# A planned order on one core: in the dilated attention, transposes of queries and keys are planned with a longer cost for the Newton steps ahead of them

## The chip, the cores and the metric

One Trainium2 chip, one of its cores. The metric is the device time of one execution of the whole program in microseconds (us). The profile records one execution; it calls the engines PE (TensorE; PEld is its weight load), DVE (VectorE), ACT (ScalarE), POOL (GpSimd) and SP (which issues the loads).

## The reference, cut to what matters

A two-layer decoder trunk on 256 tokens of width 1024, all in float32. Layer 0 is a half-step SwiGLU, then the dilated attention that this change is about, then another SwiGLU; layer 1 has the same shape with another attention. In the dilated attention three groups (dilations) each have queries, keys and values for 16 heads of 64, and queries and keys are normalized per head and rotated:

```python
def rms_norm(x, g):
    y = x * lax.rsqrt(jnp.mean(x * x, axis=-1, keepdims=True) + EPS)
    return y * g

qkv = (u @ w_qkv).reshape(b, s, N_DIL, 3, N_HEADS, HEAD_DIM)
for g in range(N_DIL):
    q = rope(rms_norm(qkv[:, :, g, 0], q_gain[g]))
    k = rope(rms_norm(qkv[:, :, g, 1], k_gain[g]))
    o, lse = dilated_attention(q, k, qkv[:, :, g, 2], DIL_WINDOWS[g], DIL_RATES[g])
# the three outputs are merged by softmax of their lse; then @ w_o
```

## The kernel before

Every float32 product is made as three products of split operands (high part of both, and the two mixed ones), so weights come in from HBM as tiles `st` of 1 MB, are rounded on ACT to `wh` (L387) and their remainder is made on DVE as `wl` (L413), six half tiles of each at a time. DVE also does the sums for the modulation (L393, one line of `w_ada` at a time) in between.

The dilated attention works on four heads at a time, so there are four rounds, called heads 0-3, 4-7, 8-11 and 12-15 below. In a round PE first projects queries and keys of group 0, then 1, then 2 (`project`: 48 matmuls of 512 columns, lines 849 to 851, into two PSUM tiles, one for each 128 tokens), then values of two groups (48 matmuls of 512 columns) and of the third (48 of 256 columns; the first round has these from earlier). After each projection of queries and keys `qk_task` runs: ACT squares the result (L860), DVE multiplies it by the rope tables (L890, L894), POOL adds the two halves (L895), DVE sums the squares by head (L864) and makes a first guess of the reciprocal root (L877, L879), POOL refines it in three Newton rounds of four small instructions each (L581, L584, L585, L586: 128x16 elements) and multiplies the rows by it (L938, one instruction for each 128 tokens), and then PE transposes the eight blocks (L906) and ACT copies them out of PSUM (L912, 128x2x128).

When all three groups of a round are transposed, its four units start (`dil_unit`: two pairs of heads by two halves of the queries). A unit makes scores on PE (L967, L969), adds mask and takes the maximum on DVE (L975, L980), exponentials on ACT (L983), the division on DVE (L989, L991), eight transposes on PE (L906 too), which ACT (L912, 128x512) and DVE (L914) copy out, and the product with values on PE (L1007). The units of one round stand between the projections of the next; those of the last round stand between its value projections and the first parts of the output projection (L466 to L468).

Every engine runs its instructions in the order in which they are written. That order is made while the program is built by a planner: `_Clock` holds a time `now` for PE and one for each of the others. A step of a task that is a generator says with `yield T` that its next step is due at T; `tick` moves `now` on by the cost of the matmuls just written and writes the steps that are due. `on(engine, ns, after)` adds a cost to an engine's time and gives back when it ends; `G(512)` adds 2.2 x 512 + 120 ns for POOL. Weights are split by the same planner (`fill`), when DVE and ACT are free by its times. For the transposes there are two PSUM tiles `tp`, for scores two (`sc`), for projections three (`mm`).

Of the kernel before, what the change touches and what calls it, by code (L numbers as in the profile page):

```python
# [223 lines left out]
class _Kernel:  # L224
# [194 lines left out]
    def fill(self):  # L419

        clk = self.clk
        while not self.hold:
            T = clk.now + self.slack
            if self.lows and self.lows[0][0][2] < clk.now + self.lag and clk.free["V"] < T:
                self.low()
# [6 lines left out]
            e = self.queue[self.qpos][0]  # L432
            if self.staged[self.qpos][1] > T:
                return
            if e[0] == "w":
                if len(self.halves) >= self.released + self.depth or clk.free["A"] > T:
                    return
            elif clk.free["V"] > T:
                return
# [159 lines left out]
    def modulated(self, gs, sh, timed=False):  # L599
# [22 lines left out]
        self.hold = False  # L622
        T = self.clk.on("V", 800 * KC, self.clk.now)
        self.clk.free["A"] = max(self.clk.free["A"], T)
# [294 lines left out]
    def qk_task(self, ps, q, k, g):  # L919

        nc = self.nc
        x = self.small(16, "qkx")
        R = []
        clk = self.clk
        sq = [self.head_squares(ps[tt], 8) for tt in range(TT)]
        for tt in range(TT):
            clk.A(512, clk.now)
            T = clk.G(512, clk.V(1280, clk.now))
            R.append(self.rope(ps[tt].rearrange("p (a r d) -> p a r d", r=4, d=HD),
                               self.dtab[g][:, 0, tt], self.dtab[g][:, 1, tt]).rearrange("p a r d -> p (a r) d"))  # L930
        for tt in range(TT):
            self.head_sums(x[:, tt * 8:(tt + 1) * 8], sq[tt])
            T = clk.V(512)
        rs = self.head_rstd(x, 16)
        T = clk.on("G", 1700, clk.on("V", 400, T))
        for tt in range(TT):
            T = clk.G(512)
            nc.gpsimd.tensor_tensor(out=R[tt], in0=R[tt],  # L938
                                    in1=rs[:, tt * 8:(tt + 1) * 8].unsqueeze(2).to_broadcast([P, 8, HD]),
                                    op=ALU.mult)  # L940
        yield T
        for tt in range(TT):
            c = slice(tt * P, (tt + 1) * P)
            self.transpose4((q[:, :, c], k[:, :, c]), R[tt].rearrange("p h d -> p (h d)"))
# [915 lines left out]
```

## Time and profile before

| | |
|---|---|
| runs of the kernel before | 1300.01, 1301.76 and 1302.33 us, median 1301.76 |
| the profiled execution's own time | 1301.44 us |
| its span, from the first to the last instruction | 1299.7 us |
| PE busy | 1219.7 us, 94% |
| DVE busy | 975.8 us, 75% |
| ACT busy | 646.0 us, 50% |
| POOL busy | 258.0 us, 20% |

The median is the middle of three runs without a profile; the rows further down are of one execution with the profile. Times in rows count from the start of its span, which is 1.7 us shorter than the execution's own time. A busy share is over the whole span, and an engine with a low share can still be the one that others wait for in one stage. The dilated attention stands in the rows from about 236 to 561 us.

### The profile page before, as it was taken

The page shows a single profiled execution, that of the slowest core. Times are in us where ns is not written, and L with a number is a line of the kernel's source. Part 1 is how long each engine was busy: PE and PEld are TensorE (multiplying, and loading weights), DVE is VectorE, ACT ScalarE, POOL GpSimd, SP SyncE. Part 2 cuts the span into 40 slices and gives each one's busy share as a digit, 9 for nine tenths or more (in the row PEclk, how much of TensorE's full clock was granted, in tenths as well). Part 3 has the DMA queues.
Part 4 walks back from the last instruction along what each step waited for, and adds up shares of the span by engine and source line. Part 5 has one row for each costly group of instructions (what it writes and reads, how often), then busy time and mean ns, then how long its engine had stood idle before and what let it go on. Part 6 is the DMA issues. An engine that isn't in the chain of part 4 may idle for free.

```text
span 1299.7 us, 23375 instructions
## 1 busy us (share of the span) xinstructions
PE 1219.7 (94%) x9373; PEld 1140.8 (88%) x9373; DVE 975.8 (75%) x1743; ACT 646.0 (50%) x1126; POOL 258.0 (20%) x356
## 2 busy tenths in 40 slices
PE   4799999789989898899999999999999889999998
PEld 3799999667777687799999999989998778999998
DVE  6799886866758677578888878878878997766652
ACT  4545454435445354456455446545435477654431
POOL 3480010462433525210000100030001353000000
PEclk9999999999899899899999999999999899999999
DMA  8889886543454534245988956776883003466650
GB/s 323 285 328 353 314 317 259 201 163 154 143 191 151 196 130 162 97 163 181 340 321 324 341 213 244 279 279 248 343 305 135 33 2 132 163 257 232 242 192 17
DMA packets 42733, 284.50 MB, mean 219 GB/s; under 512 B 5249, under 2 KB 6273, under 8 KB 9346
## 3 DMA queue, kind: packets, MB, share of 16 engines
q1 hardware_dynamic: 42626, 283.02, 58.9%
q8 instruction: 73, 1.20, 0.4%
q14 instruction: 34, 0.28, 0.1%
HBM read 281.96 MB, written 1.05 MB: 218 GB/s over the span
## 4 chain that ended last, share of the span: by engine, by line
PE 73%; DVE 12%; POOL 9%; ACT 3%; issue 2%; DMA 1%; SPq 0%; ACTq 0%; DVEq 0%; POOLq 0%
PE mm L466 18%; PE mm L467 18%; PE mm L468 18%; PE mm L849 3%; PE mm L850 3%; PE mm L851 3%; DVE wl L413 2%; POOL y L938 2%; PE tp L906 2%; POOL rs_t L584 2%; POOL rs_t L581 2%; POOL rs_y L586 2%; POOL rs_t L585 1%; DVE y L1455 1%; DVE st L393 1%
## 5 line engine op out<-in xcount | busy, mean ns | idle before, releaser
L413 DVE TENSOR_TENSOR wl<-st,wh 128x1024 fp32r<-128x1024 f32 x361 | 436.1, 1234 | 93.4 <-ACT wh L387 93.0
L387 ACT CAST wh<-st 128x1024 fp32r<-128x1024 f32 x361 | 369.0, 1049 | 133.8 <-PE mm L468 46.6
L466 PE MATMUL mm<-uh,wh 128*128 128x256 f32 x1304 | 364.6, 280 | 1.4 <-DVE y L738 1.4
L467 PE MATMUL mm<-uh,wl 128*128 128x256 f32 x1304 | 364.5, 280 | 0.0
L468 PE MATMUL mm<-ul,wh 128*128 128x256 f32 x1304 | 363.4, 279 | 0.0
L466 PEld LDWEIGHTS mm<-uh,wh 128*128 128x128 f32 x1304 | 245.0, 188 | 1.7 <-DVE y L738 1.6
L467 PEld LDWEIGHTS mm<-uh,wl 128*128 128x128 f32 x1304 | 245.1, 188 | 0.1
L468 PEld LDWEIGHTS mm<-ul,wh 128*128 128x128 f32 x1304 | 245.2, 188 | 0.0
L466 PE MATMUL mm<-y,wh 128*128 128x256 f32 x832 | 233.5, 281 | 0.1
L467 PE MATMUL mm<-y,wl 128*128 128x256 f32 x832 | 232.4, 279 | 0.0
L468 PE MATMUL mm<-y,wh 128*128 128x256 f32 x832 | 231.8, 279 | 0.0
L393 DVE CUSTOM_DVE_ANT_0 st<-st,cact 128x1024 f32<-128x1024 f32 x152 | 187.0, 1259 | 0.0
L466 PEld LDWEIGHTS mm<-y,wh 128*128 128x128 f32 x832 | 156.4, 188 | 1.1 <-issue 0.9
L467 PEld LDWEIGHTS mm<-y,wl 128*128 128x128 f32 x832 | 156.4, 188 | 0.0
L468 PEld LDWEIGHTS mm<-y,wh 128*128 128x128 f32 x832 | 156.4, 188 | 0.0
L849 PE MATMUL mm<-wh,uh 128*128 128x512 f32 (+1 forms) x336 | 137.1, 408 | 0.0
L850 PE MATMUL mm<-wl,uh 128*128 128x512 f32 (+1 forms) x336 | 132.4, 394 | 0.0
L851 PE MATMUL mm<-wh,ul 128*128 128x512 f32 (+1 forms) x336 | 131.7, 392 | 0.0
L524 POOL TENSOR_TENSOR y<-y 128x256 f32<-128x256 f32 x20 | 22.7, 1137 | 351.9 <-ACT y L505 351.9
L895 POOL TENSOR_TENSOR y<-y 128x512 f32<-128x512 f32 (+1 forms) x26 | 32.3, 1251 | 267.3 <-DVE y L894 157.2
L849 PEld LDWEIGHTS mm<-wh,uh 128*128 128x128 f32 x336 | 67.2, 200 | 14.2 <-issue 1.3
L851 PEld LDWEIGHTS mm<-wh,ul 128*128 128x128 f32 x336 | 66.9, 199 | 13.8
(254 smaller groups left out, 1622.0 us busy)
## 6 DMA issues: line engine op xcount, KB each, us to landing
st<-w_in SPq DMA_DIRECT2D x88, 1024.0 KB, 5.1
st<-w_ada SPq DMA_DIRECT2D x76, 1024.0 KB, 5.5
st<-w_out SPq DMA_DIRECT2D x44, 1024.0 KB, 6.4
st<-w_qk SPq DMA_DIRECT2D x24, 1024.0 KB, 4.9
st<-w_va SPq DMA_DIRECT2D x8, 1024.0 KB, 4.8
st<-w_o SPq DMA_DIRECT2D x8, 1024.0 KB, 4.9
st<-w_vb SPq DMA_DIRECT2D x4, 1024.0 KB, 5.5
st<-w_q SPq DMA_DIRECT2D x4, 1024.0 KB, 6.4
```

The costliest lines, as they stand in the source:

```text
L387: nc.scalar.copy(out=wh, in_=src)
L393: nc.vector.tensor_tensor_reduce(out=src, in0=src, in1=self.cact, scale=1.0, scalar=0.0, op0=ALU.mult, op1=ALU.add, accum_out=self.mod[:, ...
L413: (self.nc.gpsimd if eng == "G" else self.nc.vector).tensor_tensor(out=o, in0=src[:, c], in1=i.bitcast(F32), op=ALU.subtract)
L466: mm(out=out, lhsT=ah, rhs=bh, start=start, stop=False, **kw)
L467: mm(out=out, lhsT=al, rhs=bh, start=False, stop=False, **kw)
L468: mm(out=out, lhsT=ah, rhs=bl, start=False, stop=stop, **kw)
L581: eng.tensor_tensor(out=t, in0=y, in1=y, op=ALU.mult)
L584: eng.tensor_tensor(out=t, in0=t, in1=x, op=ALU.mult)
L849: mm(out=ps[tt], lhsT=uh[k][:, c], rhs=wh[:, o], start=k == 0, stop=False)
L850: mm(out=ps[tt], lhsT=uh[k][:, c], rhs=wl[:, o], start=False, stop=False)
L851: mm(out=ps[tt], lhsT=ul[k][:, c], rhs=wh[:, o], start=False, stop=k == KC - 1)
L895: (eng or nc.gpsimd).tensor_tensor(out=A, in0=A, in1=B, op=ALU.add)
```

## The change

One number in `qk_task` is changed. It is the planned cost in ns of the three Newton rounds on POOL, from which the planner works out when the transposes are due:

```diff
         rs = self.head_rstd(x, 16)
-        T = clk.on("G", 1700, clk.on("V", 400, T))
+        T = clk.on("G", 6100, clk.on("V", 400, T))
         for tt in range(TT):
             T = clk.G(512)
```

The planner's time for POOL is used for nothing else in this stage. With the later T the task's next step, eight transposes on PE and four copies on ACT, is written later, and what was written around it moves up. No instruction of PE is added or taken away. POOL's and SP's instructions keep their order.

The first place is ACT in the round of heads 0-3. Rows L860 are the squares of a projection, L387 splits of weights, L912 with 128x2x128 the copies behind the transposes of queries and keys, L1107 the copies of values. Before:

```order
L860 ACTIVATE y<-mm 128x512 x2
L387 CAST wh<-st 128x1024 x4
L912 COPY y<-tp 128x2x128 x4
L860 ACTIVATE y<-mm 128x512 x2
L387 CAST wh<-st 128x1024 x4
L912 COPY y<-tp 128x2x128 x4
```

And with the change:

```order
L860 ACTIVATE y<-mm 128x512 x2
L387 CAST wh<-st 128x1024 x4
L860 ACTIVATE y<-mm 128x512 x2
L387 CAST wh<-st 128x1024 x2
L912 COPY y<-tp 128x2x128 x4
L387 CAST wh<-st 128x1024 x2
L860 ACTIVATE y<-mm 128x512 x2
```

The squares of group 1 and one pair of splits stand ahead of the copies of group 0 now; on PE 18 matmuls of 512 columns moved ahead of the transposes of group 0, and 21 and 3 more stand ahead of those of groups 1 and 2.

The second place is PE where the units of heads 0-3 stand in the projections of heads 4-7, at the transposes of group 0 of heads 4-7. L849 to L851 are the projection, L967 and L969 the scores of a unit, L1007 its product with values. Before, where the first row L906 is of queries and keys and the second of a unit:

```order
L906 MATMUL tp<-ident,y 128x128 x8
L849 MATMUL mm<-wh,uh 128x512
L850 MATMUL mm<-wl,uh 128x512
L851 MATMUL mm<-wh,ul 128x512
L906 MATMUL tp<-ident,y 128x128 x8
L967 MATMUL sc<-y 128x256
L969 MATMUL sc<-y 128x128 x2
L967 MATMUL sc<-y 128x256
L969 MATMUL sc<-y 128x128 x2
L1007 MATMUL o<-y 64x128 x8
```

With the change, where the sixteen are the unit's eight and then those of queries and keys:

```order
L967 MATMUL sc<-y 128x256
L969 MATMUL sc<-y 128x128 x2
L967 MATMUL sc<-y 128x256
L969 MATMUL sc<-y 128x128 x2
L906 MATMUL tp<-ident,y 128x128 x16
L849 MATMUL mm<-wh,uh 128x512
L850 MATMUL mm<-wl,uh 128x512
L851 MATMUL mm<-wh,ul 128x512
L1007 MATMUL o<-y 64x128 x8
```

Both pairs of transposes stand together, behind the next unit's scores. ACT at the same place, before (L983 are the exponentials, L912 with 128x512 the copy of one half of a unit's transposes):

```order
L387 CAST wh<-st 128x1024 x2
L912 COPY y<-tp 128x2x128 x4
L912 COPY y<-tp 128x512
L983 ACTIVATE y,den<-y,nb 128x512 x2
L860 ACTIVATE y<-mm 128x512 x2
```

and with the change:

```order
L387 CAST wh<-st 128x1024 x2
L983 ACTIVATE y,den<-y,nb 128x512 x2
L912 COPY y<-tp 128x512
L912 COPY y<-tp 128x2x128 x4
L860 ACTIVATE y<-mm 128x512 x2
```

The next unit's exponentials stand ahead of both copies. The third place is PE at the transposes of group 2 of heads 4-7. Rows with 128x512 are the values of two groups, with 128x256 those of the third. Before:

```order
L850 MATMUL mm<-wl,uh 128x512
L851 MATMUL mm<-wh,ul 128x512
L906 MATMUL tp<-ident,y 128x128 x8
L849 MATMUL mm<-wh,uh 128x512
L850 MATMUL mm<-wl,uh 128x512
L851 MATMUL mm<-wh,ul 128x512
L849 MATMUL mm<-wh,uh 128x256
```

and with the change:

```order
L850 MATMUL mm<-wl,uh 128x256
L851 MATMUL mm<-wh,ul 128x256
L906 MATMUL tp<-ident,y 128x128 x8
L849 MATMUL mm<-wh,uh 128x256
L850 MATMUL mm<-wl,uh 128x256
```

The transposes stand behind the rest of the first value projection and behind 24 of the 48 matmuls of the second.

Counted in the same listing, this is PE's work between the end of the projection of a group and its transposes ("a" is a matmul of 512 columns, "b" one of 256, T eight transposes, S the scores and O the product of a unit):

| heads, group | before | with the change |
|---|---|---|
| 0-3, 0 | 36a | 54a |
| 0-3, 1 | 45a | 6a T 60a |
| 0-3, 2 | 45a | 18a T 30a |
| 4-7, 1 | 27a T 6a O | 3a T 21a O 33a |
| 4-7, 2 | 45a | 9a T 39a 24b |
| 8-11, 1 | 30a T 6a O | 30a T 9a O 18a |
| 8-11, 2 | 45a | 9a T 39a 33b |
| 12-15, 1 | 3a T 21a O 12a | 3a T 21a O 33a |
| 12-15, 2 | 42a | 9a T 39a 24b |

At the end of the stage the listing has 18 matmuls of the output projection between the last unit's transposes and its product before, and 3 with the change; behind that product the rest of the first three columns of the output projection follows in both.

## Rows read from the trace of the kernel before

**Rows 1.** The page's first part: busy time, share of the span and number of instructions by engine.
```profile
PE 1219.7 (94%) x9373; PEld 1140.8 (88%) x9373; DVE 975.8 (75%) x1743; ACT 646.0 (50%) x1126; POOL 258.0 (20%) x356
```

**Rows 2.** Who waited for whom, PE alone, in the stretch of the dilated attention: us in total, times, longest.
```profile
PE tp L906 <- POOL y L938: 34.3, 15, 7.6
```

**Rows 3.** Busy time by stretch (from:to, length, busy time and count of instructions by engine, granted clock of PE, share of the DMA engines, GB/s): the stage, and the 4 us behind its longest wait.
```profile
236.00:561.00 325.00, 288.64 (x1612) 233.81 (x1611) 221.79 (x402) 143.65 (x259) 135.08 (x192) 0.94 0.44 163
258.00:262.00 4.00, 3.43 (x12) 2.85 (x13) 0.10 (x1) 1.79 (x5) 1.52 (x2) 0.50 0.93 358
```

**Rows 4.** The timeline of PE at transposes of queries and keys: start, us, what, and in brackets the idle time before it and what ended it. Heads 0-3: the first three; 4-7: the next three; 8-11: two; 12-15: two.
```profile
258.57 2.11 PE L906 MATMUL tp<-ident,y 128*128 128x128 f32 x8 [7.60 <-POOL y L938]
...
278.14 0.66 PE L906 MATMUL tp<-ident,y 128*128 128x128 f32 x4 [3.24 <-POOL y L938]
...
295.35 0.66 PE L906 MATMUL tp<-ident,y 128*128 128x128 f32 x4 [2.81 <-POOL y L938]
...
348.56 2.12 PE L906 MATMUL tp<-ident,y 128*128 128x128 f32 x8 [3.03 <-POOL y L938]
...
369.80 0.66 PE L906 MATMUL tp<-ident,y 128*128 128x128 f32 x4 [3.23 <-POOL y L938]
370.80 0.65 PE L906 MATMUL tp<-ident,y 128*128 128x128 f32 x4 [0.34 <-POOL y L938]
...
428.20 0.66 PE L906 MATMUL tp<-ident,y 128*128 128x128 f32 x4 [1.56 <-POOL y L938]
...
448.77 0.66 PE L906 MATMUL tp<-ident,y 128*128 128x128 f32 x4 [3.24 <-POOL y L938]
...
508.63 2.12 PE L906 MATMUL tp<-ident,y 128*128 128x128 f32 x8 [3.44 <-POOL y L938]
...
527.01 0.66 PE L906 MATMUL tp<-ident,y 128*128 128x128 f32 x4 [3.16 <-POOL y L938]
```

**Rows 5.** The timeline of PE at full clock: the first and the last of 51 matmuls of 512 columns without a wait between them; the first and the last of 33 of 256 columns; and eight transposes, the first of six matmuls, the product of a unit, and the first of the next scores.
```profile
262.84 0.40 PE L849 MATMUL mm<-wh,uh 128*128 128x512 f32 x1
...
274.50 0.40 PE L851 MATMUL mm<-wh,ul 128*128 128x512 f32 x1
...
375.29 0.28 PE L849 MATMUL mm<-wh,uh 128*128 128x256 f32 x1
...
379.07 0.28 PE L851 MATMUL mm<-wh,ul 128*128 128x256 f32 x1
...
465.60 1.03 PE L906 MATMUL tp<-ident,y 128*128 128x128 f32 x8
466.39 0.48 PE L849 MATMUL mm<-wh,uh 128*128 128x512 f32 x1
...
467.95 1.09 PE L1007 MATMUL o<-y 128*64 128x128 f32 x16
468.98 0.70 PE L967 MATMUL sc<-y 64*128 64x256 f32 x2
```

**Rows 6.** The same behind two of the waits: the first and the last of 60 matmuls of 512 columns, and of 54.
```profile
350.32 0.78 PE L849 MATMUL mm<-wh,uh 128*128 128x512 f32 x1
...
366.17 0.40 PE L851 MATMUL mm<-wh,ul 128*128 128x512 f32 x1
...
510.40 0.78 PE L849 MATMUL mm<-wh,uh 128*128 128x512 f32 x1
...
523.46 0.39 PE L851 MATMUL mm<-wh,ul 128*128 128x512 f32 x1
```

**Rows 7.** The timeline of POOL: the first, the eighth and the ninth of the twelve Newton instructions for heads 0-3, group 0, and the product behind them; the first one and the product for heads 4-7, group 2.
```profile
247.04 1.12 POOL L581 TENSOR_TENSOR rs_t<-rs_y 128x16 f32<-128x16 f32 x1 [0.32 <-DVE rs_y L879]
...
255.14 1.07 POOL L586 TENSOR_TENSOR rs_y<-rs_t,rs_y 128x16 f32<-128x16 f32 x1
256.29 0.21 POOL L581 TENSOR_TENSOR rs_t<-rs_y 128x16 f32<-128x16 f32 x1
...
257.48 2.04 POOL L938 TENSOR_TENSOR y<-y,rs_y 128x512 f32<-128x512 f32 x2
...
359.92 1.15 POOL L581 TENSOR_TENSOR rs_t<-rs_y 128x16 f32<-128x16 f32 x1 [0.39 <-DVE rs_y L879]
...
368.70 2.04 POOL L938 TENSOR_TENSOR y<-y,rs_y 128x512 f32<-128x512 f32 x2
```

**Rows 8.** The timeline of DVE in the same stretches: the last splits of weights ahead of group 1 of heads 0-3, and the splits beside the Newton steps of heads 4-7, group 2, with the next one behind them.
```profile
253.77 2.36 DVE L413 TENSOR_TENSOR wl<-st,wh 128x1024 fp32r<-128x1024 f32 x2
...
359.77 2.38 DVE L413 TENSOR_TENSOR wl<-st,wh 128x1024 fp32r<-128x1024 f32 x2
...
364.38 2.38 DVE L413 TENSOR_TENSOR wl<-st,wh 128x1024 fp32r<-128x1024 f32 x2
...
374.21 2.36 DVE L413 TENSOR_TENSOR wl<-st,wh 128x1024 fp32r<-128x1024 f32 x2 [7.45 <-ACT wh L387]
```

**Rows 9.** The timeline of PE and ACT in heads 8-11, where a unit's transposes stand behind the next unit's scores, and ACT's copy behind that unit's exponentials.
```profile
400.88 0.70 PE L967 MATMUL sc<-y 64*128 64x256 f32 x2
...
402.49 1.09 PE L906 MATMUL tp<-ident,y 128*128 128x128 f32 x8
...
405.03 0.56 ACT L912 COPY y<-tp 128x512 f32<-128x512 f32 x1
...
405.64 1.09 PE L1007 MATMUL o<-y 128*64 128x128 f32 x16 [0.67 <-ACT y L912]
```

## The prediction

> **What bounds the kernel now.** The page first: PE is busy 94% of the span and no other engine over 75% [rows 1], so what can be won is PE's idle time and the time in which its clock is low. Next, who PE waits for, in the stage that the change touches. In the 325 us from 236 to 561, PE is busy 288.6 at a mean granted clock of 0.94 [rows 3], so 36.4 us are idle, and 34.3 of these are one wait, in 15 pieces: transposes of queries and keys wait for POOL's product L938 [rows 2]. Then the places. The timeline has nine of them: all three groups of heads 0-3, and groups 1 and 2 of the other rounds. The first costs 7.60 us, seven others about 3 us, one 1.56 with a second piece behind it [rows 4]. Behind each PE finds its clock lower: in the 4 us behind the longest wait the granted clock is 0.50, the 1.2 GHz level [rows 3]. Behind the dilated attention PE goes on with products that it is busy with nearly all the time, so a us won in the stage is a us of the kernel.
>
> What is late there is POOL. Twelve Newton instructions took 10.4 us for heads 0-3, group 0 (257.48 - 247.04) and 8.8 for heads 4-7, group 2 (368.70 - 359.92) [rows 7]; the planner had 1.7.
>
> **What the change does to the waits.** It removes no work. It puts more matmuls ahead of the transposes, so a wait shrinks by what moved ahead, as long as POOL is ready at the same time after its projection as before. Prices at full clock: a matmul of 512 columns (a) takes (274.50 - 262.84)/50 = 0.233 us, one of 256 (b) (379.07 - 375.29)/32 = 0.118, eight transposes (T) 466.39 - 465.60 = 0.79, a unit's product (O) 468.98 - 467.95 = 1.03 [rows 5]. Work before plus wait before is the time from the end of a projection until its product L938 is there; I call it the lag. Work between, by the table in the section on the change:
>
> - Heads 0-3, group 0: 36a (8.4) and 7.60. 18a more are 4.2, which leaves a wait of 3.4.
> - Group 1: 10.5 + 3.24 = 13.7. With the change 6a, that wait of 3.4, T and 60a stand between, over 19 us: no wait.
> - Group 2: 10.5 + 2.81, and about 1.0 that low clock cost within the 45a: 14.3. Now 18a T 30a = 12.0: a wait of 2.3. Nothing but these values can cover it, since the units need all three groups.
> - Heads 4-7, group 1: 9.5 + 3.03 = 12.5 against 15.1 now. Group 2: 10.5 + 3.23 = 13.7 against 14.8.
> - Heads 8-11: 10.2 + 1.56 = 11.8 against 15.1; 13.7 against 15.9.
> - Heads 12-15: 10.2 + 3.44 = 13.7 against 15.1; 9.8 + 3.16 = 13.0 against 14.8 [rows 4, 5].
>
> So the last six go to nothing, with margins of 1.1 to 3.3 us, and the first three come to 5.7.
>
> **A new wait.** At group 0 of heads 4-7, which waited for nothing worth naming, sixteen transposes stand together. The two PSUM tiles are taken by the unit's eight, and the first of them is free when ACT has copied it, but ACT has the next unit's exponentials first. The trace shows that order once, in heads 8-11: transposes at 402.49, the copy ends at 405.03 + 0.56 = 405.59, and PE's next user, the unit's product, waits 0.67 [rows 9]. There six matmuls stood between; here the next eight transposes come 0.79 behind the first and wait until 3.1 behind them: 2.4 us with the signal. Bounds: 0, if DVE gets to the mask that much earlier, and 3.1. I take 2.4. Behind the wait the unit's product, its successor's transposes and group 1's matmuls are late by as much, and nothing else.
>
> **Sum of waits.** 34.3 before, 5.7 + 2.4 = 8.1 after: 26.2 us won.
>
> **What goes with the waits.** Two more terms. First, where PE waits, the second four transposes wait for the second L938. In two places that lies inside one row of eight: 350.32 - 348.56 = 1.76 in place of 0.79 [rows 4 to 6], 1.0 each; in five others a first four takes 1.00 less 0.34 of counted idle time in place of half of 0.79 [rows 4], 0.26 each. Together 3.2. Second, the low clock: 60a behind a wait took 366.17 - 350.32 = 15.85 us where 59 x 0.233 = 13.76 are due, 2.1 lost; 54a behind another took 13.06 for 12.36, 0.7 lost [rows 6]. Seven waits go; with the middle of the two, 1.4, that is 9.8, and with the ends 4.9 to 14.7. The new wait may bring one such loss: 0 to 2.1, taken as 1.4.
>
> **What it costs.** At the end of the stage 15 of the 18 matmuls between the last unit's transposes and its product are gone: 15 x 0.118 = 1.8 us of cover, of which copies that take 0.56 on ACT [rows 9] and a signal need only a part. I take 1.0, between 0 and 2.5 (the split of the last product behind it may show too). Last, DVE. It is busy 221.8 us in the stage [rows 3]; in 289 that is 77%, so it is not the bound, but between two projections it makes four splits and two modulation sums, 366.76 - 359.77 = 7.0 us [rows 8], and the rope chain, which with the 8.8 of Newton and 1.0 of L938 taken from a lag of 13.7 is 3.9: 10.9 of PE's 12.0 (48a and T). A few short waits for a split or for a late first guess are likely. I take 2.0 over the stage, between 0 and 6. SP's order is the same, and so are the loads; they come when DVE frees a tile, a little sooner.
>
> Sum: 26.2 + 3.2 + 9.8 - 1.4 - 1.0 - 2.0 = 34.8 us. The profiled execution's own time is 1301.4 (0.3 under the median of 1301.8, so nothing is to be scaled): **1267 us**, its own range 1259 to 1276 by the ends of the clock term and of the costs.
>
> **A rule against it.** A Newton instruction takes no fixed time. From 247.04 to 255.14 seven of them came at 1.157 us each; the ninth took 0.21, at 256.29, just when DVE's splits ended (253.77 + 2.36 = 256.13) [rows 7, 8]. DVE then stood idle, because PE did. So the chain is at its fastest exactly while PE waits for it, and a PE that doesn't wait keeps DVE splitting.
>
> The Trainium skill, SBUF — State Buffer, section "Who interferes with whom", says that a DVE instruction with two inputs in SBUF and a GpSimd instruction that reads SBUF share one port, and that whichever comes second is blocked until the other is over. The trace agrees, with 1.16 us beside the splits and 0.21 without. By that rule alone, all twelve steps would take DVE's pace once PE keeps going, which is the first rival; by the rows, the sum above.
>
> **Rivals.**
>
> *Newton steps at DVE's pace, slower than before.* Twelve at 1.157 are 13.9 instead of 8.8, lags of 13.7 become 18.8 (heads 0-3, group 0, eight of whose steps were slow already: plus 3.5). Waits: 6.9, 0, 7.4 for heads 0-3, then 3.7, 4.0, 3.7, 2.9, 3.7, 4.0 and the new 2.4: 38.7, which is 4.4 more than now; clock and second fours are not won, the new low clock (1.4) and the end (1.0) are paid: 1308, and up to 1318 if each L938 waits for a split too (nine at 1.1). It decides from a chain of some 13 us on. For it: the rows just named. Against: DVE's order holds about six splits and sums between the first guess of one group and the rope of the next (four and two in the stretch of [rows 8]), so only about six steps can be slow, as in the 8.8; and the next split, at 374.21, waits for ACT [rows 8].
>
> *Half of that.* Nine slow steps and three at 0.3: 11.3, lags longer by 2.5. The margins of 1.1 to 2.2 are gone at four or five places, 4.5 us; heads 0-3, group 2 wait 2.5 more; each wait brings a low clock of 1.4 back, 7: 14 less won, 1281. For it: in the new order a pair of ACT's splits stands ahead of the copies that it stood behind, so DVE's following splits can fall into the chain. Against: values must be projected first to free their tiles.
>
> *The wait moves to the weights.* DVE's 10.9 of 12.0 grow past 12 when POOL holds a split up or DVE waits for squares; PE then waits 1.5 us at each of twelve projections: 18 less won, 1285. For it: the stretch of [rows 8] is all work. Against: six halves of each kind are made ahead, and in this stage none of PE's waits that count is for a split [rows 2, 3].
>
> **Chances.** The forecast 0.70; half the Newton rival 0.13; weights 0.08; Newton at DVE's pace 0.05; better than 1257, with a larger clock term and no costs, 0.04. About 0.2%, 2.6 us, is what a measurement of this kernel can tell. Faster by more than that 0.92, the first three and the last but for a little; within it 0.03, the edge of the slow-Newton rival; slower 0.05. The range from 1257 to 1285 takes in the forecast's own, the half rival and most of the weights; it leaves out the slower rival, the better case and some edges, about 0.2.
>
> **What would show it.** In the profile after, PE's wait for L938 should be about 6 us in at most four or five pieces, at heads 0-3, groups 0 and 2, and nothing of 3 us in the other rounds; one new wait of about 2.4 for ACT's copy at heads 4-7, group 0; a stage of about 290 us at a granted clock of 0.97 or more; Newton chains of up to 9 us, from first instruction to L938. It is wrong if those chains grow past 11 us, if PE waits for DVE's splits, or if waits of 3 us are at the same nine places. Outside the stage nothing should change.

## The result, and the profile after

The changed kernel takes 1270.24 us, the median of four runs from 1269.18 to 1271.57. The kernel before, run beside it, takes 1302.05 (1300.01 to 1304.17). The ratio is 0.9759, with a 95% interval from 0.9743 to 0.9774, so 31.8 us are won. The profiled execution of after has an own time of 1271.57, the longest of the four, and a span of 1269.5, which is 30.2 shorter than that of before.

The page's first line, which answers to [rows 1]: PE has 8.4 us less busy time with the same number of matmuls, and POOL has 7.3 us more with the same number of instructions.

```profile
PE 1211.3 (95%) x9373; PEld 1134.9 (89%) x9373; DVE 981.9 (77%) x1743; ACT 644.7 (51%) x1126; POOL 265.3 (21%) x356
```

Where the time went is seen best between two fixed points of PE's program: the first projection of the dilated attention (L849) and the first matmul of the stage behind it (L543). Before:

```profile
230.52 0.40 PE L849 MATMUL mm<-wh,uh 128*128 128x512 f32 x1
...
579.00 0.95 PE L543 MATMUL tp<-ones,y 128*128 128x1 f32 x8
```

And after:

```profile
231.83 0.40 PE L849 MATMUL mm<-wh,uh 128*128 128x512 f32 x1
...
550.49 0.95 PE L543 MATMUL tp<-ones,y 128*128 128x1 f32 x8
```

The stage took 579.00 - 230.52 = 348.5 us and now takes 550.49 - 231.83 = 318.7: 29.8 less. The rest of the span was 1299.7 - 348.5 = 951.2 and is 1269.5 - 318.7 = 950.8. All of it was won in the stage.

Who PE waits for there, in the stretch that answers to [rows 2] (us in total, times, longest):

```profile
PE tp L906 <- POOL y L938: 10.3, 8, 3.4
PE tp L906 <- ACT y L912: 2.2, 1, 2.2
PE o L1007 <- ACT y L912: 1.4, 2, 0.7
```

And the stretch itself, with the columns of [rows 3]: 294 us at a granted clock of 0.97 in place of 325 at 0.94, with 15.2 us of PE idle in place of 36.4.

```profile
236.00:530.00 294.00, 278.83 (x1600) 226.87 (x1599) 228.70 (x404) 142.66 (x257) 142.87 (x192) 0.97 0.49 183
```

The places, from the timeline of PE (they answer to [rows 4]): the first two fours are heads 0-3, group 0, the next two group 2; then heads 4-7, group 0, with a unit's eight ahead of the eight of queries and keys, and the second four of heads 4-7, group 2; last both fours of heads 8-11, group 2, and the second four of heads 12-15, group 2.

```profile
259.92 0.66 PE L906 MATMUL tp<-ident,y 128*128 128x128 f32 x4 [3.41 <-POOL y L938]
260.92 1.12 PE L906 MATMUL tp<-ident,y 128*128 128x128 f32 x4 [0.34 <-POOL y L938]
...
287.08 0.66 PE L906 MATMUL tp<-ident,y 128*128 128x128 f32 x4 [2.23 <-POOL y L938]
288.08 1.12 PE L906 MATMUL tp<-ident,y 128*128 128x128 f32 x4 [0.34 <-POOL y L938]
...
325.26 1.09 PE L906 MATMUL tp<-ident,y 128*128 128x128 f32 x8
328.56 1.66 PE L906 MATMUL tp<-ident,y 128*128 128x128 f32 x8 [2.21 <-ACT y L912]
...
363.46 0.65 PE L906 MATMUL tp<-ident,y 128*128 128x128 f32 x4 [1.03 <-POOL y L938]
...
434.22 0.66 PE L906 MATMUL tp<-ident,y 128*128 128x128 f32 x4
436.20 0.66 PE L906 MATMUL tp<-ident,y 128*128 128x128 f32 x4 [1.33 <-POOL y L938]
...
505.07 0.66 PE L906 MATMUL tp<-ident,y 128*128 128x128 f32 x4 [1.30 <-POOL y L938]
```

The reader is to see three things. The waits of 3 us at the first four transposes are gone from every round but the first, where 3.41 and 2.23 are left. In three places the second four wait 1.0 to 1.3 where nothing had been foreseen: the first four start at once, the second product comes late. (The eighth piece of the wait for L938 is 0.34, at the second four of heads 8-11, group 1.) And there is one new wait, for ACT. ACT's own timeline shows what the copy stood behind: the two halves of the next unit's exponentials, whose first waited for DVE's maximum.

```profile
326.43 0.72 ACT L983 ACTIVATE y<-y,nb 128x512 f32<-128x512 f32 x1 [4.74 <-DVE nb L980]
...
327.86 0.56 ACT L912 COPY y<-tp 128x512 f32<-128x512 f32 x1
```

POOL at heads 4-7, group 2, the place of the last rows of [rows 7]:

```profile
351.58 1.15 POOL L581 TENSOR_TENSOR rs_t<-rs_y 128x16 f32<-128x16 f32 x1 [0.39 <-DVE rs_y L879]
...
358.60 0.20 POOL L585 TENSOR_SCALAR rs_t<-rs_t 128x16 f32<-128x16 f32 x1
...
360.38 3.02 POOL L938 TENSOR_TENSOR y<-y,rs_y 128x512 f32<-128x512 f32 x2
```

And DVE beside it:

```profile
360.82 3.67 DVE L413 TENSOR_TENSOR wl<-st,wh 128x1024 fp32r<-128x1024 f32 x2 [2.40 <-ACT wh L387]
```

These splits follow a pair of ACT's, which now stands ahead of the copies of the transposes (they begin at 362.47). Before, ACT's pair at this place stood behind the copies, at 373.07:

```profile
359.73 2.00 ACT L387 CAST wh<-st 128x1024 fp32r<-128x1024 f32 x2
```

Of the twelve steps six are slow (358.60 - 351.58 = 7.02, or 1.17 each) and six are quick (1.78, 0.30 each): 8.8 in all, as before at this place. Then the splits of DVE, which stood idle for 2.40, begin 0.44 us behind the first product. The pair of products takes 3.02 in place of 2.04, and the pair of splits 3.67 in place of 2.36 [rows 7, 8]. The second product ends at 363.40, and PE's second four start at 363.46.

### The profile page after: what moved, and what is told of

Read it like the earlier page. It is cut to its first block, busy times and chain, and to the rows that moved or that the text cites. A ratio compares the mean times of both kernels' runs of the same rounds, so it can differ in the third digit from the quotient of the medians.

```text
span 1269.5 us, 23369 instructions
## 1 busy us (share of the span) xinstructions
PE 1211.3 (95%) x9373; PEld 1134.9 (89%) x9373; DVE 981.9 (77%) x1743; ACT 644.7 (51%) x1126; POOL 265.3 (21%) x356
## 3 DMA queue, kind: packets, MB, share of 16 engines
HBM read 281.96 MB, written 1.05 MB: 223 GB/s over the span
## 4 chain that ended last, share of the span: by engine, by line
PE 73%; DVE 14%; POOL 5%; ACT 4%; issue 2%; DMA 1%; SPq 0%; ACTq 0%; DVEq 0%; POOLq 0%
PE mm L466 18%; PE mm L467 18%; PE mm L468 18%; PE mm L849 3%; DVE wl L413 3%; PE mm L850 3%; PE mm L851 3%; DVE st L393 2%; PE tp L906 1%; PE o L1007 1%; DVE y L1455 1%; POOL y L938 1%; POOL rs_t L581 1%; PE sc L967 1%; POOL rs_t L584 1%
## 5 line engine op out<-in xcount | busy, mean ns | idle before, releaser
L387 ACT CAST wh<-st 128x1024 fp32r<-128x1024 f32 x361 | 368.9, 1048 | 133.0 <-PE mm L468 48.8
L849 PE MATMUL mm<-wh,uh 128*128 128x512 f32 (+1 forms) x336 | 133.4, 397 | 0.0
L850 PE MATMUL mm<-wl,uh 128*128 128x512 f32 (+1 forms) x336 | 129.1, 384 | 0.0
L851 PE MATMUL mm<-wh,ul 128*128 128x512 f32 (+1 forms) x336 | 128.7, 383 | 0.0
L849 PEld LDWEIGHTS mm<-wh,uh 128*128 128x128 f32 x336 | 64.3, 191 | 14.3 <-issue 1.8
L275 ACT CAST y<-y 128x256 fp32r<-128x256 f32 x88 | 35.8, 406 | 80.2 <-DVE y L738 78.4
```

The costliest lines, as they stand in the source:

```text
L275: self.nc.scalar.copy(out=hi, in_=src)
L387: nc.scalar.copy(out=wh, in_=src)
L849: mm(out=ps[tt], lhsT=uh[k][:, c], rhs=wh[:, o], start=k == 0, stop=False)
L850: mm(out=ps[tt], lhsT=uh[k][:, c], rhs=wl[:, o], start=False, stop=False)
L851: mm(out=ps[tt], lhsT=ul[k][:, c], rhs=wh[:, o], start=False, stop=k == KC - 1)
```

## The experiments

The theory: PE waited for a chain of Newton steps that the planner took for far too short, and matmuls moved ahead of the transposes cover it. The rivals: the gain comes from the order as such (for instance from DVE and ACT working further ahead), or POOL falls to DVE's pace once PE keeps going. The runs came in three groups, each with runs of the kernel before beside it: medians 1301.06 for the first four below, 1300.53 for the next four, 1299.99 for the last three. Ratios are to these.

### One Newton round in the order of before

```diff
-        rs = self.head_rstd(x, 16)
+        rs = self.head_newton(x, self.head_seed(x, 16), 16, None, 1)
```

(`head_newton` gets a fifth argument, the number of rounds, here and in the next experiment and the one with four rounds.)

> The order of the kernel before, instruction for instruction on PE, but one Newton round in place of three for queries and keys (two rounds, that is part of the computation, are left out). Theory of the waits: the change won by PE no longer waiting for POOL, so a chain shorter by eight instructions (lags of 13.7 to about 9.5 us against covers of 9.5 to 10.5) wins about the same without moving a transpose: waits of PE for L938 of 34 us fall to 5 or less, time 1255 to 1266. Rival: the moved order itself (splits and squares earlier on ACT and DVE) won the time; then this stays near 1290 to 1300.

Measured: 1265.0 us (1264.08 to 1266.93), ratio 0.9721 (0.9700 to 0.9742). The waits of PE in the stage:

```profile
PE tp L906 <- POOL y L938: 13.3, 11, 2.7
```

With the old order and a shorter chain the kernel is as quick as with the new order, or quicker, so the moved order is not needed for the gain. That it adds nothing of its own in the changed kernel is not shown by this run; but of PE's 36.4 us of idle time before, all waits other than that for L938 come to 2.1, so little else was there for an order to win. The 13.3 us that are left miss what was expected. POOL's timeline at heads 0-3, group 2 says why:

```profile
280.15 1.15 POOL L581 TENSOR_TENSOR rs_t<-rs_y 128x16 f32<-128x16 f32 x1 [0.39 <-DVE rs_y L879]
...
284.83 3.88 POOL L938 TENSOR_TENSOR y<-y,rs_y 128x512 f32<-128x512 f32 x2
```

All four steps that are left are slow ones (284.83 - 280.15 = 4.7 us), since the quick ones were those behind the splits, and the two products now fall into the splits and take 3.88 instead of 2.04. Leaving out two thirds of the steps shortens the lag by about 8.8 + 2.0 - 4.7 - 3.9 = 2.2 us only.

### One Newton round in the changed order

The same edit with the planner's 6100.

> The changed order with one Newton round (two left out). Theory of the waits: what the changed kernel still waits for POOL (10.3 us, with some 4 us of low clock behind it) goes, the 2.2 us for ACT's copy at heads 4-7, group 0 stays: 1254 to 1259. Rival, POOL no longer matters after the change: 1268 to 1271.

Measured: 1256.6 us (1254.46 to 1260.59), ratio 0.9658 (0.9632 to 0.9685). PE's wait for L938 is down to one piece, and the new wait for ACT stands as it was:

```profile
PE tp L906 <- ACT y L912: 2.2, 1, 2.2
PE tp L906 <- POOL y L938: 1.3, 1, 1.3
```

By the two ratios, (0.9759 - 0.9658) x 1301 = 13 us of the changed kernel's time are still due to the two other rounds. The wait for ACT stays at 2.2 with a short chain, so it does not come from POOL's chain: it is made by the order.

### The Newton steps on DVE, in the order of before

```diff
-        rs = self.head_rstd(x, 16)
+        rs = self.head_rstd(x, 16, nc.vector)
```

DVE needs three instructions for a round, so nine take the place of POOL's twelve.

> The order of the kernel before, all three Newton rounds on DVE (nine instructions of 128x16) in place of POOL. If the port that POOL shares with DVE's splits makes the chain long, the chain falls from 8.8 to about 2 us, lags from 13.7 to about 7.5, no wait for L938 is left, and DVE pays some 2 us for each of twelve chains under cover: 1252 to 1262, less than the changed kernel. Rival, DVE becomes the bound (10.9 us of work for 12.0 of PE between two projections become 12.9): PE waits for splits instead, 1265 to 1280.

Measured: 1261.32 us (1259.61 to 1263.10), ratio 0.9691 (0.9668 to 0.9715), the lowest median of all kernels here that do the whole computation, and below the changed kernel's 0.9759 with no overlap of the intervals. The waits of PE:

```profile
PE tp L906 <- DVE y L991: 4.4, 6, 1.4
...
PE tp L906 <- POOL y L938: 1.9, 4, 0.8
```

DVE at heads 0-3, group 0, the first of the nine and the splits behind them; then the division of a unit at two places:

```profile
248.51 0.18 DVE L581 TENSOR_TENSOR rs_t<-rs_y 128x16 f32<-128x16 f32 x1
...
250.28 6.32 DVE L413 TENSOR_TENSOR wl<-st,wh 128x1024 fp32r<-128x1024 f32 x4
...
382.48 2.54 DVE L991 TENSOR_SCALAR y<-y,rd 128x512 f32<-128x512 f32 x2
...
390.62 0.88 DVE L991 TENSOR_SCALAR y<-y,rd 128x512 f32<-128x512 f32 x2
```

And POOL behind the nine:

```profile
250.51 3.88 POOL L938 TENSOR_TENSOR y<-y,rs_y 128x512 f32<-128x512 f32 x2 [2.28 <-DVE rs_y L589]
```

The chain takes 250.51 - 248.51 = 2.0 us where it took 10.4 [rows 7]. With no number of the planner changed, PE's wait for L938 falls from 34.3 to 1.9. What it costs is seen in the same rows: the products run beside the splits at once, the four splits take 6.32, and the transposes of the units now wait 4.4 in six pieces for DVE's division, which is 2.54 long at some places.

### The planned cost at 7500 instead of 6100

```diff
-        T = clk.on("G", 1700, clk.on("V", 400, T))
+        T = clk.on("G", 7500, clk.on("V", 400, T))
```

> The changed kernel with 7.5 us planned for the Newton steps instead of 6.1. By its order PE has 1.2 to 2.1 us more work ahead of most transposes (14.7 for heads 0-3, group 0, still 12.0 for group 2, 15.9 to 17.3 for groups 1 and 2 of the others). Theory of the waits: the second four transposes' waits of 1.0 to 1.3 us go, and 2 us of the first wait: 1264 to 1268. Rival, later transposes push the units together and cost more than they win: 1272 to 1280.

Measured: 1263.26 us (1261.33 to 1265.51), ratio 0.9712 (0.9687 to 0.9737): better than 6100, and not told apart from the chain on DVE. PE waits, in all and at its longest place, which is heads 0-3, group 2:

```profile
PE tp L906 <- POOL y L938: 8.1, 5, 5.5
```

```profile
285.64 2.12 PE L906 MATMUL tp<-ident,y 128*128 128x128 f32 x8 [5.55 <-POOL y L938]
```

Beside this one 2.6 us in four pieces are left, where 6100 left 7.7 in six. The later number covers a longer chain too: at heads 8-11, group 2, POOL took 11.4 us from first step to L938 (415.81 to 427.23), nine slow steps and three quick ones. It can't cover heads 0-3, group 2: nothing but the values stands between its projection and the units. The wait there grew from 2.23 to 5.55, since PE comes to these transposes at 285.64 - 5.55 = 280.1 instead of 284.8, while POOL's product starts at 284.55 instead of 285.98: DVE, which has the rope and the first guess to do, has hardly any idle time left in the 20 us ahead of that guess (19.7 busy).

### The new number in the first round only, and in the others only

`qk_task` is given the round `hg`, and the number is chosen by it; the second kernel has the two numbers exchanged.

```diff
-    def qk_task(self, ps, q, k, g):
+    def qk_task(self, ps, q, k, g, hg):
-        T = clk.on("G", 1700, clk.on("V", 400, T))
+        T = clk.on("G", 6100 if hg == 0 else 1700, clk.on("V", 400, T))
```

> 6.1 us planned for heads 0-3 alone, 1.7 for the rest, so the order is that of the changed kernel up to the units of heads 0-3 and that of the kernel before from there. Theory of the waits, by the two traces: its three waits go from 14.3 to 6.3 us, and the low clock behind the last of them was longer in the changed kernel: 6 to 9 us won, 1293 to 1296. Rival, the rounds are not independent and the moved start shifts what follows: 1285 or 1300.

> The reverse: 1.7 us for heads 0-3, 6.1 for the others. If the two parts add up, this wins what the first does not: 23 to 26 of the 31.8 us, 1275 to 1279. The wait of 2.2 us for ACT's copy at heads 4-7, group 0 is in it.

Measured: 1291.81 us (1287.20 to 1293.24), ratio 0.9924 (0.9902 to 0.9947) with the first round alone, and 1279.76 (1277.46 to 1281.16), ratio 0.9832 (0.9814 to 0.9850) with the others alone. The gains are 1300.53 - 1291.81 = 8.7 and 20.8 us, 29.5 together beside the 31.8 of the whole change; by the ratios, each against its own runs of before, 0.76% and 1.68% beside 2.41%. Within the intervals, some 0.2% on either side of each, the first round and the others add up. The waits for L938, first the first round alone, then the others alone:

```profile
PE tp L906 <- POOL y L938: 26.4, 13, 3.7
```

```profile
PE tp L906 <- POOL y L938: 18.3, 9, 7.6
PE tp L906 <- ACT y L912: 2.2, 1, 2.2
```

From 34.3 the first round takes 7.9 us of waits and the others 16.0. The wait for ACT comes with the others, as it should.

### Four Newton rounds in the changed order

The same edit of `head_newton`, with four rounds and 6100: twelve steps become sixteen.

> The changed order with a fourth Newton round, four more POOL instructions in each chain (added work, the result is only more exact). Theory that only some six of the instructions are slow, since DVE's order has six splits and sums there: the four more take 0.3 us each, chains of 8.8 become 10.0, waits for L938 grow from 10.3 to about 18, time 1276 to 1282. Rival, every instruction takes DVE's pace once PE keeps going: chains of 8.8 become 13.4, waits of 3 us are back at eight places, 1295 to 1305.

Measured: 1284.48 us (1279.47 to 1288.75), ratio 0.9873 (0.9840 to 0.9905), between what the theory and what the rival gave. POOL at heads 8-11, group 2, step 14 of the sixteen:

```profile
440.52 1.14 POOL L584 TENSOR_TENSOR rs_t<-rs_t,qkx 128x16 f32<-128x16 f32 x1
```

Where DVE idles, four more steps cost 1.2 us (heads 0-3, group 0: 11.6 for 10.4); here three of them fell into DVE's next splits, and the chain, up to L938, grew from 8.8 to 12.6. Both prices exist, and the order of DVE's splits against the chain decides place by place which is paid.

### The old number at heads 4-7, group 0, alone

```diff
-        T = clk.on("G", 1700, clk.on("V", 400, T))
+        T = clk.on("G", 1700 if hg == 1 and g == 0 else 6100, clk.on("V", 400, T))
```

This takes the new wait for ACT away and leaves the rest.

> The changed kernel with 1.7 us at one place, group 0 of heads 4-7, so that its transposes stand ahead of the unit's again, as before the change. If the 2.2 us wait there comes from ACT's order (the next unit's exponentials ahead of both copies), it goes, with up to 1.5 us of low clock: 1266 to 1268. Rival, the wait moves to the next transposes: 1270 to 1271.

Measured: 1270.73 us (1268.42 to 1274.53), ratio 0.9771 (0.9747 to 0.9796), not told apart from the 0.9759 of the changed kernel. The wait for ACT is gone, and the waits for L938 grew from 10.3 to 12.3: at group 2, two groups on, the second four waited 1.0, and now the whole eight wait. PE at heads 4-7, group 2:

```profile
358.29 2.12 PE L906 MATMUL tp<-ident,y 128*128 128x128 f32 x8 [3.22 <-POOL y L938]
```

POOL there (three of the steps and the products) and DVE:

```profile
345.84 1.15 POOL L581 TENSOR_TENSOR rs_t<-rs_y 128x16 f32<-128x16 f32 x1 [0.39 <-DVE rs_y L879]
...
352.85 0.20 POOL L585 TENSOR_SCALAR rs_t<-rs_t 128x16 f32<-128x16 f32 x1
...
353.44 1.07 POOL L581 TENSOR_TENSOR rs_t<-rs_y 128x16 f32<-128x16 f32 x1
...
357.19 2.04 POOL L938 TENSOR_TENSOR y<-y,rs_y 128x512 f32<-128x512 f32 x2
```

```profile
353.19 3.56 DVE L413 TENSOR_TENSOR wl<-st,wh 128x1024 fp32r<-128x1024 f32 x3 [0.50 <-ACT wh L387]
```

The chain turned quick at 352.85, when DVE ran out of rounded weights. At 353.19 it had them again, and the next three steps are slow once more: nine slow and three quick, 357.19 - 345.84 = 11.35 us, which is the prediction's second rival (11.3) at one place (the six of the start, then three of 1.05 to 1.08). In the changed kernel the same splits waited for ACT until 360.82 and met the products instead of the steps.

### DVE's chain with a later plan

The Newton steps on DVE as above, with a planned cost of 3000 and of 6100.

> Newton steps on DVE (the chain took 2.0 us there, 248.51 to 250.51 in the first such kernel), with 3.0 us planned for them instead of 1.7, so transposes stand 1.1 to 1.6 us later than in the kernel before. Theory: what that kernel still waits at transposes (6.3 us for L938 and for DVE's divisions, which POOL's product holds up) goes for the most part, the 1.9 us for a split and 1.9 for a projection's PSUM tile may stay: 1255 to 1260. Rival, its waits are DVE's load and not the place of the transposes: 1260 to 1263.

> Newton steps on DVE in the order of the changed kernel. If the place of the transposes has slack to spare now, nothing is left of POOL's waits, and the 2.2 us for ACT's copy at heads 4-7, group 0 is back: 1256 to 1261. Rival, late transposes cost elsewhere (units together at the end of the stage): 1262 to 1266.

Measured: 1262.56 us (1261.08 to 1264.44), ratio 0.9714 (0.9693 to 0.9736), and 1267.29 (1265.61 to 1268.45), ratio 0.9746 (0.9729 to 0.9763). With 3000 the rival came: the waits for DVE's division stay, 4.3 us in seven pieces. With 6100 the time lies above what either gave. With a chain of 2 us a later plan wins nothing, and the order of the changed kernel costs some 7 us against the plan of 1700 (0.55% of 1300). With 6100 the longest wait is one of a projection for DVE's rope, which is late behind it:

```profile
PE mm L849 <- DVE y L894: 3.4, 2, 3.3
```

### The planned cost at 9000

> Newton on POOL, 9.0 us planned. The waits for L938 are down to heads 0-3, group 2 (12.0 us of cover in every one of these orders, 2 to 6 us of wait) at 7.5 us planned, so more can win 1 us at most, and the units of the last round are pushed to the end of the stage, with few matmuls of the output projection between them: 1264 to 1270, slower than with 7.5 us. Rival, later is better still: 1258 to 1262.

Measured: 1267.05 us (1264.88 to 1271.53), ratio 0.9749 (0.9724 to 0.9775). The waits for L938 are the fewest of all orders with POOL's full chain, and yet by the ratios the time is some 5 us above that with 7500, with intervals that overlap a little, so that 9000 is the slower one is likely and not shown:

```profile
PE tp L906 <- POOL y L938: 6.8, 3, 5.6
PE o L1007 <- ACT y L912: 3.1, 3, 2.1
```

More than half of the wait is that of heads 0-3, group 2, which no number covers, and the units' products wait more for ACT. Over 1700, 6100, 7500 and 9000 the ratios are 1, 0.9759, 0.9712 and 0.9749.

## Why the prediction was right, and which terms were off

The profiled pair won 29.8 us in the stage: 36.36 - 15.36 = 21.0 of it is PE's idle time between the two points above, and 8.8 is work of PE that took less time. The prediction had 26.2 - 1.0 - 2.0 = 23.2 and 3.2 + 9.8 - 1.4 = 11.6, together 34.8.

**What bounds the kernel: right.** One Newton round in the old order, the chain on DVE and the late transposes are three unlike edits that each take PE's wait for L938 down, to 13.3, 1.9 and 10.3, and each win 32 to 40 us.

**Heads 0-3: right.** 3.4 and 2.3 were predicted at groups 0 and 2, and 3.41 and 2.23 came. Group 1 waits for nothing. The way of counting, work moved ahead against a lag that stays, holds here, because the lag stays: from the end of the projection to the start of L938 it was 15.3 and 13.6 us at these two groups before, and is 15.4 and 13.4.

**The other six places: the waits of the first four are gone, but the lag did not stay.** The prediction's condition, POOL as early after its projection as before, failed at all six. From the end of the projection to the start of L938, in us, and beside it the margin that the forecast's sum left:

| heads, group | before | after | margin |
|---|---|---|---|
| 4-7, 1 | 10.80 | 12.12 | 2.6 |
| 4-7, 2 | 12.80 | 13.44 | 1.1 |
| 8-11, 1 | 10.05 | 14.46 | 3.3 |
| 8-11, 2 | 12.81 | 14.90 | 2.2 |
| 12-15, 1 | 12.13 | 13.27 | 1.4 |
| 12-15, 2 | 12.02 | 13.72 | 1.8 |

It grew by 11.3 in all, and most at heads 8-11, group 1, where the chain took 5.53 us before (420.71 to 426.24), two of its steps slow, and takes 9.05 with six slow:

```profile
409.47 0.22 POOL L581 TENSOR_TENSOR rs_t<-rs_y 128x16 f32<-128x16 f32 x1 [0.39 <-DVE rd L989]
...
418.52 2.05 POOL L938 TENSOR_TENSOR y<-y,rs_y 128x512 f32<-128x512 f32 x2
```

Longer chains are 6.9 of the 11.3. The rest lies ahead of the chain: at heads 8-11, group 2, the first guess starts 5.9 us behind the projection where it started 3.8 behind it. At heads 8-11, group 1, the 4.4 are more than the margin of 3.3; the first four still start at once, at 419.62, because nothing holds the products up there this time (2.05 for the pair, 3.88 before). That the first four wait nowhere in these rounds was therefore in part luck: the forecast had assumed no growth, and the growth used up nearly all of the margins.

For the second four they were not enough. The margins of 1.1 to 3.3 were taken with a pair of products of 2.04. At group 2 of the three rounds a pair of ACT's splits of weights stands ahead of the copies, as the second rival says, so DVE's next splits start while POOL multiplies, and the pair takes 3.02, 3.91 and 3.03. The second four wait 1.03, 1.33 and 1.30 us there; how much of that is the held-up product and how much the longer lag was not separated. With three pieces of 0.34, where the second four follow a product that nothing holds up (2.04 or 2.05 for the pair), 4.7 of the 10.3 us that PE waits for L938 are waits of second fours, and the term of these waits, 5.7 in the forecast, came to 10.3. The argument that the half rival drew on was right, but at group 2 it struck the products and not the Newton steps.

**The new wait for ACT: right.** 2.4 was predicted, 2.21 came, at the place named and behind the exponentials named. In the run that takes it away, PE's waits for L938 grew by 2.0, so nearly all of it came back elsewhere.

**The costs: too high as waits.** For the end of the stage and for DVE 1.0 + 2.0 was taken. What PE waits for beside L938 and the copy went from 36.4 - 34.3 = 2.1 to 15.4 - 10.3 - 2.2 = 2.9, so these came to 0.8; two waits of a unit's product for ACT, 0.7 each, are the largest part, where before had one. PE waits for no split. What DVE's fuller work cost is in the lags above.

**The clock: right in sign, and short in the profiled execution by what one place lost.** PE's busy time fell by 8.8 where 11.6 was forecast. The place is the work behind the wait at heads 0-3, group 2. Ten us behind it after, and at the like place before:

```profile
287.00:297.00 10.00, 9.58 (x31) 7.33 (x32) 2.51 (x8) 5.10 (x11) 1.02 (x2) 0.55 0.17 70
```

```profile
294.00:304.00 10.00, 8.30 (x37) 6.37 (x38) 1.48 (x5) 5.18 (x13) 2.22 (x3) 0.83 0.29 118
```

The granted clock is 0.55 over 10 us in place of 0.83, though PE was busy for 9.58 of them: 10 x (0.83 - 0.55) = 2.8 us of full-speed work. The prediction took the same loss, 1.4, for each wait whether it stayed or not.

An estimate for the whole stage, PE's busy time in steps of 1 us times what the granted clock is short of 1: the low clock cost 18.4 us before, 1.5 to 3.4 behind each of the nine places, and 8.3 after, behind three: 1.6 and 5.0 at heads 0-3, groups 0 and 2, and 1.7 behind the wait for ACT. So the seven waits that went gave back 14.6, more than the 9.8 and 3.2 taken for them. (Most of the 3.2 is clock too: the second four of heads 0-3, group 2, waiting for nothing more, took 0.77, from 288.08 to 288.85, where half of 0.79 is due.) But 3.3 were lost again at group 2, which makes 10.0 in all; why the busy time fell by 1.2 less than that was not followed.

That loss is not a fixed price of this order. In the kernel with the old number at heads 4-7, group 0, nothing is changed up to this place; PE waited 2.71 here, and the like ten us have 0.83:

```profile
286.30:296.30 10.00, 9.81 (x44) 7.71 (x45) 3.66 (x9) 5.98 (x11) 1.13 (x2) 0.83 0.19 75
```

So it differs from execution to execution, and here it went against the forecast. The other runs of after, at mean clocks of 0.986 to 0.991 where the profiled one had 0.985, are 0.5 to 2.1 us shorter in span. By the medians the miss is 34.8 - 31.8 = 3.0 us, inside the forecast's own range; in the profiled pair it is 5.0, of which 2.2 are idle time and 2.8 PE's busy time.

**The rule against it: borne out, and it took only part of its price.** The Trainium skill, SBUF — State Buffer, section "Who interferes with whom", says that either engine blocks the other, by which comes first. The traces agree in both directions: a step takes 1.05 to 1.25 us beside DVE's splits and sums and 0.20 to 0.29 without, and two splits take 3.67 beside the products and 2.36 without. What kept the chains at 8.8 is that DVE has only so much work between the first guess and the wait for ACT: six slow steps at heads 4-7, group 2. In the changed kernel the rule took its price at group 1 of the later rounds and group 2 of the last, 0.8 to 3.5 us of chain, under cover. Where the limit was shifted (heads 4-7, group 0 early; planned 7500 at heads 8-11, group 2) or the chain was made longer (four rounds), it took 2.5 to 3.8 us at a place. Newton wholly at DVE's pace, the rival that ends slower than before, was seen nowhere; nine slow steps of twelve is the most. (That rival's list of waits took a lag of 18.8 at all six later places. With 5.1 added to the sum's own lags of 12.5, 11.8 and 13.0, three of them are 2.5, 1.8 and 3.3, and the total is 35.2 instead of 38.7: 1305 instead of 1308.)

What would show it: the new wait for ACT, the clock of 0.97, chains of up to 9 us (9.05, but 10.45 at heads 0-3, group 0, as before) and nothing outside the stage (0.4 us) came as written. The stage of about 290 us came as some 295 (325 - 29.8). "At most four or five" pieces of the wait for L938 did not: there are eight.

## What to carry to other kernels

Before a stall is covered with moved work, the same stall is worth a look at its source: here nine instructions on an engine that is the busier by far (2.0 us for the chain) do at least as well as the best plan tried around twelve on an idle one (8.8 us; 0.9691 and 0.9712 are not told apart), because the idle engine's steps wait for the busy one's instructions anyway. Where an order is set by planned costs, a cost that the trace contradicts by a factor of five is a good place to start, and the best number is found by trying some on both sides, since a plan that covers one place can uncover another. And when a consumer takes a producer's result in halves, both halves need a margin, with the producer's duration taken beside its neighbours and not alone.

## What the runs showed of the hardware that was not expected

POOL's large products hold DVE up by about as much as DVE holds them up, 1.7 and 1.8 us at the same place: four splits took 6.32 us beside two products and 4.66 without (the row of before is below), and the two products 3.88 beside the splits and 2.04 without; two divisions of a unit (L991) took 2.54 at 382.48, beside two products, and 0.88 at 390.62 in the same kernel, without. The kernel with the chain on DVE pays this and wins all the same.

```profile
246.87 4.66 DVE L413 TENSOR_TENSOR wl<-st,wh 128x1024 fp32r<-128x1024 f32 x4
```

A small POOL instruction of 128x16 took 1.05 to 1.25 us or 0.20 to 0.29 in the stage of the kernels before and after, and nothing between, so the length of a chain is set by the number of its steps that fall beside DVE's splits and sums.

After a wait of 2.2 us the clock stayed low for some 10 us although PE was then busy, while behind the wait of 3.4 us at group 0 of the same execution it was back within 4 (0.58 from 260 to 264, and 1.00 in the next 4). Neither the place nor the length of the wait decides which comes. At the same place it was 0.50, 0.50 and 0.74 in the three stretches of 4 us from 285 to 297 behind 5.55 us (planned 7500), but 0.82 over ten us behind 5.64 (planned 9000) and 0.83 behind 2.71 (the row above). What does decide stays open; no run here was made for it.
